# The last feature block by halves of the tokens, without Pool

## The chip, the cores and the metric

The kernel runs on one core of a Trainium2 chip. The metric is the device time of that core in microseconds, the median of several runs. The engines are TensorE (PE in the profile, with PEld for its weight loads), VectorE (DVE), ScalarE (ACT), GpSimd (POOL) and SyncE (SP), which issues all the DMAs here.

## What is computed

One layer of a diffusion backbone over 256 latent tokens and 256 context tokens, 1024 features wide: a gated feed-forward half step, a token mixer of retention and Fourier branches, a second gated feed-forward half step for the latent tokens, and a norm over the features. The change touches the end of it:

```python
x = x + 0.5 * g3x * swiglu(modulate(rmsnorm(x, norm_ffn2[l]), sh3x, sc3x), w13_ffn2[l], w2_ffn2[l])
...
return rmsnorm(x, norm_final)

def swiglu(h, w13, w2):
    a, b = jnp.split(h @ w13, 2, axis=-1)
    return (jax.nn.silu(a) * b) @ w2

def rmsnorm(x, w):
    xf = x.astype(jnp.float32)
    y = xf * lax.rsqrt(jnp.mean(xf * xf, axis=-1, keepdims=True) + EPS)
    return (y * w.astype(jnp.float32)).astype(x.dtype)
```

The hidden width of the feed-forward part is 2816.

## The kernel before

Features lie on the 128 partitions and tokens along the free axis. The 1024 features are `KT` = 8 blocks, the hidden width `MT` = 22 blocks of 128. The residual stream is `xs[j]`, 128 partitions by 512 columns, context tokens first and latent tokens behind (`T` = 256 each).

All large products are made from three fp32r products (`mm3`, lines 95 to 97): the weights and the moving operand are each split into a high and a low part, and low weights by high data, high by low, and high by high are summed in PSUM. A product loads its 128x128 weights anew each time. `load_w` brings weights in: a DMA on SP (line 84), a cast on ScalarE (line 85), a subtraction on VectorE (line 86). Squares are summed over the features by a product with `ones`, in plain f32; such a product leaves two records in the trace.

The last stage is the second matrix of the second feed-forward part. For each feature block `j`, `w2_chunks` brings 22 blocks of weights in three pieces, 66 products of 256 columns fill the bank `z`, and `y_evac` (line 467, VectorE) adds it, times a gate, to `xs[j]`. For the blocks 0 to 6, `add_sq` then squares the block (line 461, ScalarE) and adds the square to `ssum` (line 462, VectorE), and ScalarE writes the block times its norm weight to `xw` (line 1052). All of that lies beside the products of the next block. For block 7 nothing comes after: the sum of the seven squares goes through PE in the middle of its products (line 1047), and then one thing follows the other. ScalarE squares the last block (line 1054), PE adds that to the sum (line 1055), `rstd_of` takes the root on ScalarE (line 233) and the reciprocal on VectorE (line 235), and `xw` is multiplied by it in three groups of blocks, 6 and 7 on Pool, 0 to 2 and 3 to 5 on VectorE (line 1061), each stored by a DMA of its own (line 1062).

Two other places show up below. Line 269, in the opening, multiplies f32 data of 128 columns; line 306 multiplies f32 data of two columns; line 631 turns blocks of fp32r data over by a product with the unit matrix, in the transpose form of the product, with 128 columns. The order of the instructions on each engine is set by a scheduler when the program is built, within what the code's dependences allow.

Of the kernel before, what the change touches and what calls it, by code (L numbers as in the profile page):

```python
# [7 lines left out]
F32 = mybir.dt.float32  # L8
F32R = mybir.dt.float32r
BF16 = mybir.dt.bfloat16  # L10
AF = mybir.ActivationFunctionType
ALU = mybir.AluOpType

P = 128
T = 256
D = 1024
KT = D // P
FF = 2816
MT = FF // P
# [6 lines left out]
T2K = 4  # L26
# [8 lines left out]
BIAS, NRM, GNW, DEC = 0, 72, 104, 120  # L35
# [4 lines left out]
def block_kernel(ctx: ExitStack, tc: tile.TileContext, i: dict, out: bass.AP):  # L40
    nc = tc.nc
    V, S, G, PE = nc.vector, nc.scalar, nc.gpsimd, nc.tensor

    def pool(name, bufs=1, **kw):
        return ctx.enter_context(tc.tile_pool(name=name, bufs=bufs, reuse_waits="tile", **kw))
# [3 lines left out]
    tp = pool("tp")  # L49
# [16 lines left out]
    def bank(name):  # L66
        return psum.tile([P, 512], F32, name=name, tag="ps")
# [9 lines left out]
    def load_w(src, n, lo_engine=None, at=0):  # L77

        uid[0] += 1
        raw, hi, lo = [wtile(t, f"{t}{uid[0]}")[:, at : at + n] for t in ("wr", "wh", "wl")]  # L80
        dst = raw
        if len(src.shape) == 3:
            dst = dst.rearrange("p (k c) -> p k c", k=src.shape[1])
        nc.sync.dma_start(dst, src)
        S.copy(hi, raw)  # L85
        (lo_engine or V).tensor_tensor(lo, raw, f32(hi), op=ALU.subtract)  # L86
        return hi, lo
# [5 lines left out]
    def mm3(o, w, a, start, stop):  # L93

        PE.matmul(o, w[1], a[0], start=start, stop=False)  # L95
        PE.matmul(o, w[0], a[1], start=False, stop=False)  # L96
        PE.matmul(o, w[0], a[0], start=False, stop=stop)  # L97

    def sl(pair, *idx):
        return pair[0][idx], pair[1][idx]  # L100
# [11 lines left out]
    start = ExitStack()  # L112
# [11 lines left out]
    ones = per.tile([P, P], F32, name="ones")  # L124
# [14 lines left out]
    sm = per.tile([P, N_SMALL], F32, name="sm")  # L139
# [11 lines left out]
    xs, first_ada, first_w = [], {}, {}  # L151
# [31 lines left out]
    for n, c in enumerate(ch):  # L183
        for q in range(4):
            r = slice(32 * q, 32 * q + 1)
# [41 lines left out]
    def gate_col(st, s, k):  # L227
        return gate[:, s, st * KT + k : st * KT + k + 1]

    def rstd_of(ps_ap, width, name):  # L230

        sd = tp.tile([P, T], F32, name=f"sd{name}", tag="sd", bufs=1)
        S.activation(sd[:, :width], ps_ap, AF.Sqrt, bias=eps)
        r = tp.tile([P, T], F32, name=f"rstd{name}", tag="rstd", bufs=2)
        V.reciprocal(r[:, :width], sd[:, :width])
        return r[:, :width]
# [4 lines left out]
    for k in range(KT):  # L241
        if k < T2K:
            sq = tp.tile([P, 512], F32, name=f"sq1_{k}", tag="t2k", bufs=T2K)
        else:
            sq = stp.tile([P, 512], F32, name=f"sq1_{k}", tag=f"at{k % 2}" if k < 6 else "xr", bufs=1 + (k > 5))
# [10 lines left out]
        for q in range(4):  # L256
            PE.matmul(
                ps_st[32 * q : 32 * q + 32, :P], ones[:, :32], sq[:, q * P : (q + 1) * P],
                start=(k == 0), stop=(k == KT - 1), skip_group_check=True, tile_position=(0, 32 * q),
# [82 lines left out]
    def gated_unit(pa, pb, name):  # L342
        sa = tp.tile([P, 512], F32, name=f"sa{name}", tag="t2k", bufs=T2K)
        S.activation(sa, pa, AF.Silu)
        V.tensor_tensor(sa, sa, pb, op=ALU.mult)
        gg = (
            gp.tile([P, 512], F32R, name=f"gh{name}", tag="gh", bufs=HALF),
            gp.tile([P, 512], F32R, name=f"gl{name}", tag="gl", bufs=HALF),
        )
        split(gg[0], gg[1], sa)  # L350
        return gg
# [66 lines left out]
    g = [gated_unit(acc[2 * m], acc[2 * m + 1], f"1_{m}") for m in range(M1)]  # L418
# [25 lines left out]
    def w2_chunks(src, kts, at=0):  # L444
        ws, k0 = [], 0
        for n in kts:
            w = load_w(src[:, k0 * P : (k0 + n) * P], n * P, at=at)
            ws += [sl(w, slice(None), slice(c * P, (c + 1) * P)) for c in range(n)]
            k0 += n
        return ws  # L450

    ssum = [None]

    def add_sq(ap, cols, first, name):

        sq = tp.tile([P, 512], F32, name=f"sq{name}", tag="t2k", bufs=T2K)
        w = cols.stop - cols.start
        if first:
            S.activation(ssum[0][:, cols], ap, AF.Square)
            return  # L460
        S.activation(sq[:, :w], ap, AF.Square)
        V.tensor_tensor(ssum[0][:, cols], ssum[0][:, cols], sq[:, :w], op=ALU.add)

    def y_evac(ps, j, streams, st, col0):
        for n, s in enumerate(streams):
            c = slice(s * T, (s + 1) * T)
            V.scalar_tensor_tensor(
                xs[j][:, c], ps[:, col0 + n * T : col0 + (n + 1) * T], gate_col(st, s, j),
                xs[j][:, c], op0=ALU.mult, op1=ALU.add,
            )  # L470
# [45 lines left out]
    g = []  # L516
# [228 lines left out]
    def o_unit(hd, us):  # L745
        pss = [bank(f"o{hd}_{n}") for n in range(4)]
        for n in range(4):
            w = v_weights(hd, n)
            for k in (2 * n, 2 * n + 1):
                u = sl(us[k // 2], slice(None), slice((k % 2) * T, (k % 2 + 1) * T))  # L750
                for d in range(4):
                    c = (k % 2) * DV + d * P
                    mm3(pss[d][:, :T], sl(w, slice(None), slice(c, c + P)), u, k == 0, k == KT - 1)
        sq = [tp.tile([P, 512], F32, name=f"os{hd}_{n}", tag="t2k", bufs=T2K) for n in range(2)]
        for d in range(4):
            S.activation(sq[d // 2][:, (d % 2) * T : (d % 2 + 1) * T], pss[d][:, :T], AF.Square)
        G.tensor_tensor(sq[0], sq[0], sq[1], op=ALU.add)
        for d in range(4):
            c = slice((d % 2) * T, (d % 2 + 1) * T)
            S.copy(tt[2 * hd + d // 2][:, c], pss[d][:, :T])  # L760
        return sq[0]
# [106 lines left out]
    sq = None  # L868
    for hd in range(HEADS):
# [20 lines left out]
        sq = o_unit(hd, us)  # L890
# [19 lines left out]
    for j in range(KT):  # L910
        ws = [load_w(i["wgate"][j, c], 1024) for c in range(2)]
# [7 lines left out]
        for k in range(2 * KT):  # L919
            c = (k % 8) * P  # L920
# [33 lines left out]
    XC = slice(T, 2 * T)  # L954
# [49 lines left out]
    def raw_unit(m, pa, pb):  # L1004
        r = rstd3[0]
        cc = tp.tile([P, 2], F32, name=f"cc{m}", tag="cc", bufs=4)
        V.tensor_copy(cc[:, 0:1], pa[:, T : T + 1])
        V.tensor_copy(cc[:, 1:2], pb[:, T : T + 1])
        a = tp.tile([P, 512], F32, name=f"a2_{m}", tag="t2k", bufs=T2K)
        V.tensor_tensor(a[:, :T], pa[:, :T], r, op=ALU.mult)  # L1010
        S.activation(a[:, :T], a[:, :T], AF.Silu, bias=cc[:, 0:1])
        V.tensor_tensor(a[:, T:], pb[:, :T], r, op=ALU.mult)
        V.scalar_tensor_tensor(a[:, :T], a[:, T:], cc[:, 1:2], a[:, :T], op0=ALU.add, op1=ALU.mult)
        gg = g2_tiles(m)
        split(gg[0], gg[1], a[:, :T])
        return gg
# [11 lines left out]
    g = [raw_unit(m, *first[m]) for m in range(2)]  # L1028
# [7 lines left out]


    ssum[0] = per.tile([P, 512], F32, name="ssum4", tag="ssum")
    pf = bank("st4")
    xw = g2.tile([P, KT, T], F32, name="xw")  # L1040
    for j in range(KT):
        ws = w2_chunks(i["w2b"][j], (8, 8, 6))
        py = bank(f"z{j}")
        for k in range(MT):
            mm3(py[:, :T], ws[k], g[k], k == 0, k == MT - 1)
            if (j, k) == (KT - 1, 8):
                PE.matmul(pf[:, :T], ones, ssum[0][:, :T], start=True, stop=False)
        y_evac(py, j, (1,), 2, 0)
        if j < KT - 1:
            add_sq(xs[j][:, XC], slice(0, T), j == 0, f"4_{j}")  # L1050
            c = NRM + 3 * KT + j
            S.mul(xw[:, j, :], xs[j][:, XC], sm[:, c : c + 1])
    sq = tp.tile([P, 512], F32, name="sq4_last", tag="t2k", bufs=T2K)
    S.activation(sq[:, :T], xs[KT - 1][:, XC], AF.Square)
    PE.matmul(pf[:, :T], ones, sq[:, :T], start=False, stop=True)
    r = rstd_of(pf[:, :T], T, "4")
    c = NRM + 4 * KT - 1
    S.mul(xw[:, KT - 1, :], xs[KT - 1][:, XC], sm[:, c : c + 1])
    for j0, j1, engine in ((6, 8, G), (0, 3, V), (3, 6, V)):
        rb = r.unsqueeze(1).to_broadcast([P, j1 - j0, T])  # L1060
        engine.tensor_tensor(xw[:, j0:j1, :], xw[:, j0:j1, :], rb, op=ALU.mult)
        nc.sync.dma_start(out[:, j0:j1, :], xw[:, j0:j1, :])


# [102 lines left out]
```

## Time and profile before

| | |
|---|---|
| median of 3 runs | 988.46 us (988.08 to 989.26) |
| profiled execution, its time | 986.11 us |
| its span | 984.3 us |
| PE busy in the span | 957.3 us (97%) |
| VectorE busy | 658.1 us (67%) |
| ScalarE busy | 468.1 us (48%) |
| Pool busy | 37.7 us (4%) |

The profiled execution is one of its own and not one of the three runs. Times in the rows are microseconds from the start of its span unless marked ns. Products on PE are pipelined: the records of two of them overlap, so the spacing of their starts, and not the length of a record, is what a product costs. The chain of work that ended last is followed back from the last instruction, at each step to what released it.

### The profile page before, as it was taken

What the parts mean: (1) busy time and instruction counts of PE and PEld (TensorE: products, weight loads), DVE (VectorE), ACT (ScalarE), POOL (GpSimd) and SP (SyncE); (2) the same over time, 40 slices, a digit from 0 to 9 for tenths busy, and PEclk for the clock granted to TensorE, in tenths of its full rate; (3) what the DMA queues carried; (4) which work ended last, traced back from release to release, by engine and by line L of the source; (5) the groups of instructions that cost most, each with busy time, mean ns of one, the idle gap of its engine ahead of it and who ended that gap; (6) DMA issues with size and microseconds to landing.
All of it is one profiled execution on the core that took longest, in us unless ns stands there. A gap on an engine that the chain in (4) does not pass through costs nothing.

```text
span 984.3 us, 16732 instructions
## 1 busy us (share of the span) xinstructions
PE 957.3 (97%) x6792; PEld 881.2 (90%) x6792; DVE 658.1 (67%) x1056; ACT 468.1 (48%) x733; POOL 37.7 (4%) x21
## 2 busy tenths in 40 slices
PE   6999999999999999899999999899999999999996
PEld 4778888888888889899999999899999999999995
DVE  7879999998333433966765646975555688555553
ACT  5444322224422432755665647755444566555541
POOL 0000000000000001200000006200000000000000
PEclk9999999999999999999999999999999999999998
DMA  8757766995332232323231526356656565666661
GB/s 348 238 203 235 235 195 214 352 391 195 97 109 67 78 99 86 97 87 121 95 130 44 157 81 186 117 175 201 192 189 199 174 190 175 211 198 186 199 190 43
DMA packets 49237, 166.84 MB, mean 169 GB/s; under 512 B 5380, under 2 KB 7044, under 8 KB 49160
## 3 DMA queue, kind: packets, MB, share of 16 engines
q1 hardware_dynamic: 49160, 165.77, 52.4%
q8 instruction: 53, 0.87, 0.3%
q14 instruction: 24, 0.20, 0.1%
HBM read 164.70 MB, written 1.05 MB: 168 GB/s over the span
## 4 chain that ended last, share of the span: by engine, by line
PE 93%; DVE 3%; ACT 1%; DMA 1%; issue 1%; DVEq 0%; SPq 0%; ACTq 0%
PE y L95 4%; PE y L97 4%; PE y L96 4%; PE pa L97 4%; PE pb L95 4%; PE pa L95 4%; PE pb L97 4%; PE pa L96 3%; PE pb L96 3%; PE ro L97 2%; PE ro L95 2%; PE ro L96 2%; PE fb L97 2%; PE fa L97 2%; PE fb L96 2%; PE fa L96 2%
## 5 line engine op out<-in xcount | busy, mean ns | idle before, releaser
L86 DVE TENSOR_TENSOR wl<-wr,wh 128x1024 fp32r<-128x1024 f32 (+1 forms) x214 | 248.7, 1163 | 190.4 <-ACT wh L85 189.5
L85 ACT CAST wh<-wr 128x1024 fp32r<-128x1024 f32 (+1 forms) x226 | 227.3, 1007 | 273.7 <-PE y L97 79.2
L198 DVE CUSTOM_DVE_ANT_0 junk<-ada,cb,sm 128x1024 bf16<-128x1024 f32 x96 | 123.0, 1281 | 6.5 <-DMA ada<-in_ada 4.9
L96 PE MATMUL y<-gl,wh 128*128 128x512 f32 (+1 forms) x198 | 72.4, 366 | 0.0
L95 PE MATMUL y<-gh,wl 128*128 128x512 f32 (+1 forms) x198 | 72.3, 366 | 0.0
L97 PE MATMUL y<-gh,wh 128*128 128x512 f32 (+1 forms) x198 | 72.2, 365 | 0.0
L97 PE MATMUL pa<-h1h,wh 128*128 128x512 f32 x152 | 59.2, 389 | 0.0
L96 PE MATMUL pa<-h1l,wh 128*128 128x512 f32 x152 | 59.2, 389 | 0.0
L95 PE MATMUL pa<-h1h,wl 128*128 128x512 f32 x152 | 59.2, 389 | 0.0
L95 PE MATMUL pb<-h1h,wl 128*128 128x512 f32 x152 | 59.2, 389 | 0.0
L96 PE MATMUL pb<-h1l,wh 128*128 128x512 f32 x152 | 59.2, 389 | 0.0
L97 PE MATMUL pb<-h1h,wh 128*128 128x512 f32 x152 | 59.1, 389 | 0.0
L96 PE MATMUL z<-g2l,wh 128*128 128x256 f32 x176 | 48.8, 277 | 0.0
L97 PE MATMUL z<-g2h,wh 128*128 128x256 f32 x176 | 48.6, 276 | 0.0
L95 PE MATMUL z<-g2h,wl 128*128 128x256 f32 x176 | 48.6, 276 | 0.0
L86 POOL TENSOR_TENSOR wl<-wr,wh 128x1024 fp32r<-128x1024 f32 x12 | 29.9, 2515 | 439.2 <-ACT wh L85 439.2
L96 PEld LDWEIGHTS y<-gl,wh 128*128 128x128 f32 x198 | 37.3, 188 | 6.1
L95 PEld LDWEIGHTS y<-gh,wl 128*128 128x128 f32 x198 | 37.2, 188 | 6.0
L97 PEld LDWEIGHTS y<-gh,wh 128*128 128x128 f32 x198 | 37.2, 188 | 6.0
L97 PE MATMUL fb<-hnh,wh 128*128 128x256 f32 x144 | 39.8, 276 | 0.0
L96 PE MATMUL fb<-hnl,wh 128*128 128x256 f32 x144 | 39.8, 276 | 0.0
L97 PE MATMUL fa<-hnh,wh 128*128 128x256 f32 x144 | 39.8, 276 | 0.0
(336 smaller groups left out, 2903.1 us busy)
## 6 DMA issues: line engine op xcount, KB each, us to landing
ada<-in_ada SPq DMA_DIRECT2D x72, 512.0 KB, 5.2
wr<-in_w13b SPq DMA_DIRECT2D x44, 512.0 KB, 4.4
wr<-in_w13a SPq DMA_DIRECT2D x38, 512.0 KB, 4.4
wrv<-in_wv SPq DMA_DIRECT2D x16, 512.0 KB, 4.5
wr<-in_wg SPq DMA_DIRECT2D x16, 512.0 KB, 4.1
wr<-in_wgate SPq DMA_DIRECT2D x16, 512.0 KB, 4.4
wr<-in_pret SPq DMA_DIRECT2D x16, 512.0 KB, 4.1
wr<-in_w2b SPq DMA_DIRECT2D x16, 512.0 KB, 3.8
```

What stands on the lines that cost most here:

```text
L85: S.copy(hi, raw)
L86: (lo_engine or V).tensor_tensor(lo, raw, f32(hi), op=ALU.subtract)
L95: PE.matmul(o, w[1], a[0], start=start, stop=False)
L96: PE.matmul(o, w[0], a[1], start=False, stop=False)
L97: PE.matmul(o, w[0], a[0], start=False, stop=stop)
L198: V.tensor_tensor_reduce(junk, raw, cb[:, s, :], 1.0, sm[:, BIAS + n : BIAS + n + 1], ALU.mult, ALU.add, mod[:, s, n : n + 1],)
```

## The change

Blocks 0 to 6 of the last stage stay as they are, but for the multiplication by the norm weight, which moves into a helper. Block 7 is computed in two halves of 128 tokens. Each half has banks of its own for the product (`z7_0`, `z7_1`) and for the sum of squares (`st4_0`, `st4_1`), 66 products of 128 columns with the same weights, its own add, square, sum, root and reciprocal, and then all eight blocks of `xw` for its 128 tokens are multiplied in two groups of four, both on VectorE, and stored by two DMAs. Pool has no part in it. A store takes, on each partition, four pieces of 128 elements.

```diff
+    def weighted(j, c):
+        n = NRM + 3 * KT + j
+        S.mul(xw[:, j, c], xs[j][:, T + c.start : T + c.stop], sm[:, n : n + 1])
+
-    for j in range(KT):
+    for j in range(KT - 1):
         ws = w2_chunks(i["w2b"][j], (8, 8, 6))
         py = bank(f"z{j}")
         for k in range(MT):
             mm3(py[:, :T], ws[k], g[k], k == 0, k == MT - 1)
-            if (j, k) == (KT - 1, 8):
-                PE.matmul(pf[:, :T], ones, ssum[0][:, :T], start=True, stop=False)
         y_evac(py, j, (1,), 2, 0)
...
-    sq = tp.tile([P, 512], F32, name="sq4_last", tag="t2k", bufs=T2K)
-    S.activation(sq[:, :T], xs[KT - 1][:, XC], AF.Square)
-    PE.matmul(pf[:, :T], ones, sq[:, :T], start=False, stop=True)
-    r = rstd_of(pf[:, :T], T, "4")
-    c = NRM + 4 * KT - 1
-    S.mul(xw[:, KT - 1, :], xs[KT - 1][:, XC], sm[:, c : c + 1])
-    for j0, j1, engine in ((6, 8, G), (0, 3, V), (3, 6, V)):
-        rb = r.unsqueeze(1).to_broadcast([P, j1 - j0, T])
-        engine.tensor_tensor(xw[:, j0:j1, :], xw[:, j0:j1, :], rb, op=ALU.mult)
-        nc.sync.dma_start(out[:, j0:j1, :], xw[:, j0:j1, :])
+    j = KT - 1
+    ws = w2_chunks(i["w2b"][j], (8, 8, 6))
+    for n in range(2):
+        c = slice(n * P, (n + 1) * P)
+        py, pf = bank(f"z{j}_{n}"), bank(f"st4_{n}")
+        for k in range(MT):
+            mm3(py[:, :P], ws[k], sl(g[k], slice(None), c), k == 0, k == MT - 1)
+            if k == 12:
+                PE.matmul(pf[:, :P], ones, ssum[0][:, c], start=True, stop=False)
+        x = xs[j][:, T + n * P : T + (n + 1) * P]
+        V.scalar_tensor_tensor(x, py[:, :P], gate_col(2, 1, j), x, op0=ALU.mult, op1=ALU.add)
+        sq = tp.tile([P, 512], F32, name=f"sq4_last{n}", tag="t2k", bufs=T2K)
+        S.activation(sq[:, :P], x, AF.Square)
+        PE.matmul(pf[:, :P], ones, sq[:, :P], start=False, stop=True)
+        r = rstd_of(pf[:, :P], P, f"4_{n}")
+        weighted(j, c)
+        for j0 in range(0, KT, 4):
+            rb = r.unsqueeze(1).to_broadcast([P, 4, P])
+            V.tensor_tensor(xw[:, j0 : j0 + 4, c], xw[:, j0 : j0 + 4, c], rb, op=ALU.mult)
+            nc.sync.dma_start(out[:, j0 : j0 + 4, c], xw[:, j0 : j0 + 4, c])
```

On PE, the end of the program before. `z` is the bank of block 7, `g2h` and `g2l` the gated hidden blocks, `wh` and `wl` the two parts of the weights; the number at the end is the size of the moving operand.

```order
L97 MATMUL z_10445<-g2h_9721,wh_10440 128x256
L95 MATMUL z_10445<-g2h_9790,wl_10441 128x256
L96 MATMUL z_10445<-g2l_9791,wh_10440 128x256
L97 MATMUL z_10445<-g2h_9790,wh_10440 128x256
L1055 MATMUL st_9796<-sq_last,ones 128x256
```

On PE after the change, the place inside the products of half 1 (`z_1`) where the squares of half 0 are summed:

```order
L95 MATMUL z_1_10526<-g2h_8893,wl_10434 128x128
L96 MATMUL z_1_10526<-g2l_8894,wh_10433 128x128
L97 MATMUL z_1_10526<-g2h_8893,wh_10433 128x128
L1067 MATMUL st_0_10445<-sq_last_10514,ones 128x128
L95 MATMUL z_1_10526<-g2h_8962,wl_10434 128x128
```

The sum over the last squares stood behind all products; that of half 0 now stands behind 27 of the 66 products of half 1 (the sum of half 1 stands last, as before).

On VectorE, the end of the program before, from the last weight piece on:

```order
L86 TENSOR_TENSOR wl_10441<-wr_10439,wh_10440 128x768
L467 SCALAR_TENSOR_TENSOR xs_112<-z_10355,gate,xs_112 128x256
L462 TENSOR_TENSOR ssum_9795<-ssum_9795,sq_6_10423 128x256
L467 SCALAR_TENSOR_TENSOR xs_112<-z_10445,gate,xs_112 128x256
L235 RECIPROCAL rstd_10519<-sd_10517 128x256
L1061 TENSOR_TENSOR xw<-xw,rstd_10519 128x768 x2
```

And after the change:

```order
L462 TENSOR_TENSOR ssum_9795<-ssum_9795,sq_6_10422 128x256
L1064 SCALAR_TENSOR_TENSOR xs_112<-z_0_10444,gate,xs_112 128x128
L235 RECIPROCAL rstd_0_10519<-sd_0_10517 128x128
L1072 TENSOR_TENSOR xw<-xw,rstd_0_10519 128x4x128 x2
L1064 SCALAR_TENSOR_TENSOR xs_112<-z_1_10526,gate,xs_112 128x128
L235 RECIPROCAL rstd_1_10601<-sd_1_10599 128x128
L1072 TENSOR_TENSOR xw<-xw,rstd_1_10601 128x4x128 x2
```

Add, reciprocal and multiplies of half 0 stand ahead of those of half 1. On SP four stores stand where three stood, all behind the last weight load.

## Rows read from the trace of the kernel before

**Rows 1.** Page, part 1: busy time, share of the span, instructions of each engine.

```profile
PE 957.3 (97%) x6792; PEld 881.2 (90%) x6792; DVE 658.1 (67%) x1056; ACT 468.1 (48%) x733; POOL 37.7 (4%) x21
```

**Rows 2.** Stretches, PE alone: length, busy (records), granted clock, DMA share, GB/s.

```profile
13.20:14.20 1.00, 0.96 (x8) 1.00 1.01 406
966.00:974.00 8.00, 8.00 (x69) 1.00 0.01 2
```

**Rows 3.** Timeline of PE, first and last product of z7: start, length, record.

```profile
965.91 0.28 PE L95 MATMUL z<-g2h,wl 128*128 128x256 f32 x1
...
973.73 0.28 PE L97 MATMUL z<-g2h,wh 128*128 128x256 f32 x1
```

**Rows 4.** Chain that ended last, 973 to 985 us: start, length, what.

```profile
974.05 0.49 DVE xs L467
...
974.56 0.42 ACT sq_last L1054
...
975.03 0.71 PE st L1055 x2
...
975.77 0.48 ACT sd L233
...
976.27 1.76 DVE rstd L235
...
978.06 0.96 DVE xw L1061
979.02 1.94 DVEq L1161
```

**Rows 5.** Timeline of all engines, 978 to 984.4 us.

```profile
978.06 2.90 DVE L1061 TENSOR_TENSOR xw<-xw,rstd 128x768 f32<-128x768 f32 x2
978.17 1.97 POOL L1061 TENSOR_TENSOR xw<-xw,rstd 128x512 f32<-128x512 f32 x1 [356.07 <-DVE rstd L235]
```

**Rows 6.** Waits of SP from 975 us on: total, times, longest.

```profile
SPq L1161 <- DMA out_xT<-xw: 1.9, 1, 1.9
```

**Rows 7.** Timeline of the weight loads, 13 to 14.4 us.

```profile
13.24 0.97 PEld L269 LDWEIGHTS rs<-rstd1q,pick 128*128 128x128 f32 x8 [1.93 <-DVE rstd1q L235]
14.13 0.36 PEld L284 LDWEIGHTS tr<-unit_raw,ada 128*128 128x128 f32 x3
```

**Rows 8.** Chain that ended last, 23 to 25 us; `acc` has 512 columns.

```profile
23.74 0.12 PE tr L306 x2
23.86 0.34 PE acc L95
24.20 0.23 PE acc L96
```

**Rows 9.** Groups of weight loads by shape: busy us, mean ns, idle before.

```profile
L95 PEld LDWEIGHTS z<-g2h,wl 128*128 128x128 f32 x176 | 33.0, 188 | 0.0
...
L631 PEld LDWEIGHTS ht<-unit,h2xh 128*128 128x128 f32 x16 | 1.7, 142 | 0.0
...
L269 PEld LDWEIGHTS rs<-rstd1q,pick 128*128 128x128 f32 x8 | 1.0, 191 | 1.9 <-DVE rstd1q L235 1.9
```

**Rows 10.** Chain that ended last, 413 to 420 us.

```profile
413.85 1.16 PE ht L631 x14
```

**Rows 11.** Groups of VectorE by shape: busy us, mean ns, idle before.

```profile
L769 DVE TENSOR_TENSOR tt<-tt,rstdo 128x512 f32<-128x512 f32 x8 | 5.1, 683 | 0.0
...
L235 DVE RECIPROCAL rstd1q<-sd1q 128x128 f32<-128x128 f32 x1 | 1.0, 953 | 0.1
```

**Rows 12.** Groups of ScalarE by shape.

```profile
L233 ACT ACTIVATE sd1q<-st,eps 128x128 f32<-128x128 f32 x1 | 0.4, 368 | 1.2 <-PE st L257 1.2
```

**Rows 13.** DMAs of the whole span: issues, KB each, median us to landing.

```profile
out_xT<-xw SPq DMA_DIRECT2D x2, 384.0 KB, 2.5
...
unit_raw<-in_unit SPq DMA_DIRECT2D x1, 64.0 KB, 1.8
```

**Rows 14.** DMAs of 43 to 50 us, two loads in pieces of 1 KB.

```profile
wr<-in_w13a SPq DMA_DIRECT2D x2, 512.0 KB, 4.1
```

More of the change, by code (lines that the diff above doesn't have):

```diff
@@ L1038, in block_kernel @@
     ssum[0] = per.tile([P, 512], F32, name="ssum4", tag="ssum")
-    pf = bank("st4")
     xw = g2.tile([P, KT, T], F32, name="xw")
-    for j in range(KT):
+    def weighted(j, c):
+        n = NRM + 3 * KT + j
+        S.mul(xw[:, j, c], xs[j][:, T + c.start : T + c.stop], sm[:, n : n + 1])
+    for j in range(KT - 1):
         ws = w2_chunks(i["w2b"][j], (8, 8, 6))
@@ L1045, in block_kernel @@
             mm3(py[:, :T], ws[k], g[k], k == 0, k == MT - 1)
-            if (j, k) == (KT - 1, 8):
-                PE.matmul(pf[:, :T], ones, ssum[0][:, :T], start=True, stop=False)
         y_evac(py, j, (1,), 2, 0)
[L1049 to L1052, printed above, removed]
-    sq = tp.tile([P, 512], F32, name="sq4_last", tag="t2k", bufs=T2K)
-    S.activation(sq[:, :T], xs[KT - 1][:, XC], AF.Square)
-    PE.matmul(pf[:, :T], ones, sq[:, :T], start=False, stop=True)
-    r = rstd_of(pf[:, :T], T, "4")
-    c = NRM + 4 * KT - 1
-    S.mul(xw[:, KT - 1, :], xs[KT - 1][:, XC], sm[:, c : c + 1])
-    for j0, j1, engine in ((6, 8, G), (0, 3, V), (3, 6, V)):
-        rb = r.unsqueeze(1).to_broadcast([P, j1 - j0, T])
-        engine.tensor_tensor(xw[:, j0:j1, :], xw[:, j0:j1, :], rb, op=ALU.mult)
-        nc.sync.dma_start(out[:, j0:j1, :], xw[:, j0:j1, :])
+        add_sq(xs[j][:, XC], slice(0, T), j == 0, f"4_{j}")
+        weighted(j, slice(0, T))
+    j = KT - 1
[18 more added lines that the diff above has]
+            nc.sync.dma_start(out[:, j0 : j0 + 4, c], xw[:, j0 : j0 + 4, c])
 def _layout(a):
```

## The prediction

> **What bounds the kernel now.** The page first: PE is busy for 97% of the span and loads weights, on the row PEld, for 90% of it; Pool does next to nothing [rows 1]. The change touches only the last 18 us, so everything else is read there. In 966 to 974 us PE has no idle time at a granted clock of 1.00, its 2.4 GHz level [rows 2]. That is the last feature block, z7: its first product starts at 965.91 and its last at 973.73, 66 products of 256 columns and the two records of the sum st [rows 3]. With one more spacing of 0.113 us PE spends 7.93 us on it. What follows is a chain with one link at a time [rows 4]: VectorE adds z to xs (0.49), ScalarE squares (0.42), PE sums the squares (0.71), ScalarE takes the root (0.48), VectorE the reciprocal (1.76), then multiplies six of the eight blocks in two steps, 0.96 and 1.94 us. The second step does what the first does and takes twice as long; Pool multiplies the other two blocks from 978.17 for 1.97 us, the same stretch [rows 5]. The last store is issued after the second step, and SP then waits 1.9 us for it [rows 6]. From the start of the add at 974.05 to the end of the span at 984.3 that is 10.3 us in which PE computes for 0.7.
>
> So the end has two parts: 7.93 us limited by PE, and 10.3 us limited by a chain. The change pays in the first to shorten the second.
>
> **Part 1, the products by halves.** The 66 products of 256 columns become 132 of 128, with the same multiplications in all, but each product has its own load of 128 columns of weights, so the loads double too. The question is whether a load hides behind a product of half the length. No fp32r product in this trace has under 256 columns, so the price comes from the nearest rows. The sums by L269 have 128 columns and a weight load for each record: eight loads start from 13.24 us on, and the next one, of L284, at 14.13, so 0.89 / 8 = 0.111 us each, again at a clock of 1.00 [rows 2, 7]. These are f32 products in two records, where the product itself might hold up the next one. The products by L306 settle that: they have two columns, practically no multiplication, and yet the two records and the product behind them take 0.12 + 0.34 us where the next ones take 0.23 each, so (0.46 - 0.23) / 2 = 0.115 us each [rows 8]. A load of fp32r weights for z and a load for L269 last the same, 188 and 191 ns [rows 9]. I take from this that a new 128x128 load can start only every 0.11 us, that 256 columns (0.113) just cover it, and that 128 columns do not. Price: 0.111 us a product whatever its width, with 0.108 and 0.1135 as its ends (a little below the two rows, and the spacing of today).
>
> After the change PE runs 132 products and, ahead of the last sum, six records of st (two halves of ssum, and the squares of half 0), 138 loads: 138 x 0.111 = 15.32 us. **PE: 15.32 - 7.93 = +7.39 us**, with the ends +6.97 and +7.73. All of it lies on the path, since nothing else is late in 966 to 974.
>
> The nearest rows on the cheap side are the transposes by L631, also 128 columns with own weights in fp32r: 14 of them take 1.16 us, 0.083 each [rows 10]. Their loads last 142 ns and not 188 [rows 9], so they are another kind of load; I leave them to a rival. The Trainium skill, page "TensorE: Matmul & The Clock Gate", section "Back-to-back issue gap", gives about 81 ns per product for sustained pairs of load and product of 128 columns. By that rule PE would pay 138 x 0.081 - 7.93 = +3.2 us, an estimate from that page. It speaks against my price, the transposes agree with it, and the loads of the kind that z uses do not.
>
> **Part 2, half 0 in the cover of half 1.** In the order PE meets the squares' sum of half 0 only after 27 products of z_1, 29 records on: 3.2 us, in which VectorE's add and ScalarE's square (under 0.9 us together) are long done. So PE does not wait there. Root, reciprocal and two multiplies of half 0 then take some 3 us: they are done some 6.3 us into the 7.9 that z_1 and its sums last. VectorE is free for half 1, and the two stores of half 0 are issued 2 us before z_1 ends. Cost zero, hidden by z_1; that cover would be gone only with a spacing under 0.07 us, and would then cost about 0.6 us.
>
> **Part 3, the chain behind half 1.** Each link has 128 columns in place of 256. The add: a VectorE step of 768 elements takes 0.96 us [rows 4] and one of 512 takes 0.683 [rows 11], 1.07 ns an element, so -0.13. The root has 0.368 in its one row of 128 columns, at the opening [rows 12], against 0.48: -0.10; the square on the same engine likewise, -0.11. The sum: two records of two passes each, 128 columns less for each of two passes in the record that holds up the other, -0.21. The reciprocal has 0.953 at the opening [rows 11], against 1.76: -0.80. The two multiplies: 512 elements each at 0.683 [rows 11], back to back with 0.08 of overlap, 1.29 us, against 2.90 for the two of today [rows 5]: -1.61. This is the largest term: 1.06 of it is the slowing of the second step beside Pool (1.94 against the first one's 0.96 less the overlap), the rest fewer elements. The last store: 256 KB in pieces of 512 B where today it is 384 KB in pieces of 3 KB. The trace has 2.5 us for today's, 1.8 for 64 KB in pieces of 512 B [rows 13], and 4.1 for the two loads of 512 KB in pieces of 1 KB [rows 14]; I take 2.5 again, because bytes go down and pieces up, with ends 1.9 and 3.5. **Chain: -2.97 us**, ends -3.5 and -1.9.
>
> The store on SP comes last in its queue, and no load stands behind it. Pool's removal costs nothing elsewhere: VectorE does 2 x 512 elements a half, half of that in the cover of z_1.
>
> **Sum.** +7.39 - 2.97 = +4.42 us. Against the profiled execution, 986.11 us with a span of 984.3, that is 990.5; that execution lies 2.35 below the median of the runs, 988.46, so I add the change to the median: **992.9 us, 0.45% slower**. Its own range is 991.9 (6.97 - 3.5) to 994.3 (7.73 - 1.9).
>
> **Rivals.** Each goes by the spacing s of a 128-column product: time = 988.46 + 138 s - 7.93 - 2.97. It decides at 0.079 us: above that the change loses. All other terms are too small to turn the sign.
>
> *Faster: loads hide behind 128 columns.* If the load streams at the speed of the product, s is half of 0.113, 0.057 us. PE then pays nothing (138 x 0.057 = 7.87), and the chain's -2.97 stands, less the 0.6 us by which half 0 would now hold VectorE: -2.4, **986.1 us**. For it: 512 columns (0.23 [rows 8]) and 256 (0.113 [rows 3]) stand in the ratio of their columns, so at 256 the load shows nowhere. Against it: the two-column products at 0.115 [rows 8]. Chance 5%.
>
> *Much the same: loads as cheap as those of the transposes.* s = 0.083 gives 11.45 - 7.93 - 2.97 = +0.55, **989.0 us**. For it: the only fp32r products of 128 columns in the trace run so [rows 10]. Against it: the shorter load of those [rows 9]. The rule of the skill named above falls here, +0.3 us by its figure. Chance 9%.
>
> *Far slower: a narrow fp32r product is run as an f32 product,* in two records. L269's four products take 0.223 each [rows 7]: 132 x 0.223 + 6 x 0.111 = 30.1, so 30.1 - 7.93 - 2.97 = +19.2, **1007.7 us**. For it: every fp32r product that multiplies has at least 256 columns here, so nothing excludes it. Against it: the transposes of that type and width have one record each [rows 10]. Chance 10%.
>
> That halves do not overlap is excluded by the order: VectorE's reciprocal and multiplies of half 0 stand ahead of the add of half 1, and PE's sum of half 0 inside z_1.
>
> **How the numbers follow.** The forecast has 76%. The range goes from the rival of equal time to a little over the forecast's own top: 988.9 to 994.5, which leaves out the faster case, the f32 case and the forecast's fringes. About 0.2%, 2 us, is what a measurement of this kernel can tell from no change: s below 0.064 is faster (5%), 0.064 to 0.093 the same (9%, and 1% for a forecast with its ends against it), the rest slower (85%).
>
> **What would show it.** In the new profile: PE products of z_0 and z_1 at a spacing of 0.11 us with loads of 188 ns; z7's stretch at 15.3 us, ending near 981.1; VectorE's chain of half 0 finished before the last product of z_1; the chain after it 7.3 us long, with two multiplies of 0.69; one record for each product. A spacing of 0.08 or 0.06 proves the price wrong, 264 records instead of 132 the third rival right; a last store over 3.5 us would break the chain's term.

## The result: 993.0 us, 0.43% slower

The changed kernel takes 993.01 us in the median of 4 runs (992.15 to 993.92), the kernel before beside it 988.40 (988.08 to 989.26): a ratio of 1.0043, with a 95% interval of 1.0031 to 1.0056. The prediction, 992.9 us, and its sign hold. The profiled execution took 992.15 us with a span of 990.1.

That span is 5.8 us longer than before's, but 1.04 of this is there before the changed code runs: z7 begins at 966.95 where before has 965.91 [rows 3]. In all the profiles of this study that start lies between 965.9 and 970.8 us, in kernels that do the same work up to there, so the time of one execution says little about a change of 0.5 us. Everything below is therefore counted from z7's first product, in two pieces: to the start of the last add (products), and from there to the end of the span (chain). An experiment without a ratio was executed once, and only its trace is read.

| | products | chain | of it, from the end of the last multiply | sum |
|---|---|---|---|---|
| before | 8.14 | 10.29 | 3.38 | 18.43 |
| after | 15.56 | 7.60 | 3.64 | 23.15 |
| difference | +7.42 | -2.69 | +0.26 | +4.73 |

The page, part 1, answers to [rows 1]:

```profile
PE 966.9 (98%) x6862; PEld 891.8 (90%) x6862; DVE 657.9 (66%) x1060; ACT 469.2 (47%) x736; POOL 35.6 (4%) x20
```

PE has 70 records more and is busy for 9.6 us more: 7.42 of it in z7's stretch (15.52 against 8.10), -0.21 in the last sum, and 2.4 ahead of z7, in work that is alike in both. VectorE does as much as before, Pool one multiply less. Then stretches: the products of half 0, those of half 1, and the chain. The columns are length, then busy time (instructions) of PE, weight loads, VectorE, ScalarE and Pool, the granted clock, the DMA share and GB/s.

```profile
966.95:974.30 7.35, 7.35 (x69) 7.35 (x67) 0.94 (x3) 0.82 (x2) 0.00 (x0) 1.00 0.00 0
974.70:982.20 7.50, 7.50 (x70) 7.50 (x69) 2.59 (x4) 0.97 (x3) 0.00 (x0) 1.00 0.16 44
982.50:990.10 7.60, 0.49 (x2) 0.30 (x2) 2.60 (x4) 0.97 (x3) 0.00 (x0) 0.69 0.31 83
```

PE has no idle time in either half, at a clock of 1.00 as in [rows 2], and the load row is as full as the product row. Half as much arithmetic per product, and as many products per microsecond as before. Timeline of PE around the seam, and the last product; it answers to [rows 3]:

```profile
966.84 0.28 PE L97 MATMUL z<-g2h,wh 128*128 128x256 f32 x1
966.95 0.22 PE L95 MATMUL z<-g2h,wl 128*128 128x128 f32 x1
967.01 0.28 PE L96 MATMUL z<-g2l,wh 128*128 128x128 f32 x1
967.12 0.27 PE L97 MATMUL z<-g2h,wh 128*128 128x128 f32 x1
...
982.19 0.28 PE L97 MATMUL z<-g2h,wh 128*128 128x128 f32 x1
```

From the first to the last are 137 steps (132 products and six records of sums) in 15.24 us, 0.111 each. Only the first narrow product, behind a wide one, starts the next after 0.06. The weight loads keep their step of 0.11 across the seam: they start at 966.84, 966.95, 967.06 and 967.17.

The chain that ended last, from the last add on (start, length, what), answers to [rows 4], with SP's wait for the last store, which answers to [rows 6]:

```profile
982.51 0.36 DVE xs L1064
...
982.89 0.32 ACT sq_last L1066
...
983.25 0.50 PE st L1067 x2
...
983.78 0.38 ACT sd L233
...
984.18 0.96 DVE rstd L235
...
985.17 0.69 DVE xw L1072
985.86 0.60 DVEq L1172
```

```profile
SPq L1172 <- DMA out_xT<-xw: 2.1, 1, 2.1
```

Every link is shorter, the second multiply (on the engine's queue in the last row, 0.60) is as quick as the first, and only the wait for the store has grown, from 1.9 to 2.1.

VectorE on the way there:

```profile
978.38 0.95 DVE L235 RECIPROCAL rstd<-sd 128x128 f32<-128x128 f32 x1 [3.33 <-ACT sd L233]
979.37 1.29 DVE L1072 TENSOR_TENSOR xw<-xw,rstd 128x512 f32<-128x512 f32 x2
982.51 0.35 DVE L1064 SCALAR_TENSOR_TENSOR xs<-z,gate,xs 128x128 f32<-128x128 f32 x1 [1.85 <-PE z L97]
```

Half 0 is multiplied at 980.66, and VectorE then waits 1.85 us for the products of half 1: half 0 costs nothing.

### The profile page after: what moved, and what is told of

Its sections match the earlier page's. It is cut to its first block, busy times and chain, and to the rows that moved or that the text cites. A ratio compares the mean times of both kernels' runs of the same rounds, so it can differ in the third digit from the quotient of the medians.

```text
span 990.1 us, 16880 instructions
## 1 busy us (share of the span) xinstructions
PE 966.9 (98%) x6862; PEld 891.8 (90%) x6862; DVE 657.9 (66%) x1060; ACT 469.2 (47%) x736; POOL 35.6 (4%) x20
## 4 chain that ended last, share of the span: by engine, by line
PE 93%; DVE 2%; ACT 2%; DMA 1%; issue 1%; SPq 0%; DVEq 0%; ACTq 0%
PE y L95 4%; PE y L96 4%; PE y L97 4%; PE pa L97 3%; PE pa L96 3%; PE pb L96 3%; PE pb L97 3%; PE pa L95 3%; PE pb L95 3%; PE z L97 2%; PE z L96 2%; PE z L95 2%; PE ro L95 2%; PE ro L96 2%; PE ro L97 2%; PE fa L97 2%
## 5 line engine op out<-in xcount | busy, mean ns | idle before, releaser
L95 PE MATMUL z<-g2h,wl 128*128 128x256 f32 (+1 forms) x198 | 54.6, 276 | 0.0
L96 PE MATMUL z<-g2l,wh 128*128 128x256 f32 (+1 forms) x198 | 54.6, 276 | 0.0
L97 PE MATMUL z<-g2h,wh 128*128 128x256 f32 (+1 forms) x198 | 54.6, 276 | 0.0
```

## Experiments

### The two parts of the change, each alone

**Products only.** Halves on PE, before's tail with Pool.

```diff
+        if j == KT - 1:
+            for n in range(2):
+                c = slice(n * P, (n + 1) * P)
+                py = bank(f"z{j}_{n}")
+                for k in range(MT):
+                    mm3(py[:, :P], ws[k], sl(g[k], slice(None), c), k == 0, k == MT - 1)
...
+                V.scalar_tensor_tensor(x, py[:, :P], gate_col(2, 1, j), x, op0=ALU.mult, op1=ALU.add)
+            continue
...
```

> Block 7's products by halves alone (132 products of 128 columns, two adds); square, sum, root, reciprocal, multiplies and stores as in the kernel before, with Pool. My theory, a weight load every 0.111 us: z7's stretch is 134 records, 14.9 us against 7.9 before, and the chain from the last add on 10.16 us against 10.29 (an add of 128 columns): +6.8 us in all, 0.7% slower than before and 2.1 slower than the changed kernel. If loads hid behind 128 columns, z7 would stay at 7.9 and the whole be equal to before.

Measured: 996.14 us against 988.39, ratio 1.0075 (1.0059 to 1.0090). Products 15.32, chain 10.17, sum 25.50: +7.07 against before. With Pool still in the tail, VectorE's two multiplies take 0.96 and 1.93 us, as in [rows 4].

**Tail only.** Products of 256 columns, norm and stores by halves, no Pool.

```diff
+    py = bank(f"z{j}")
+    pfs = [bank(f"st4_{n}") for n in range(2)]
+    for k in range(MT):
+        mm3(py[:, :T], ws[k], g[k], k == 0, k == MT - 1)
...
     for n in range(2):
...
-            mm3(py[:, :P], ws[k], sl(g[k], slice(None), c), k == 0, k == MT - 1)
...
+        V.scalar_tensor_tensor(x, py[:, c], gate_col(2, 1, j), x, op0=ALU.mult, op1=ALU.add)
```

> The other part alone: block 7's products stay 66 of 256 columns, and add, square, sum, root, reciprocal, multiplies and stores go by halves without Pool. z7's stretch 7.9 us as before. Chain: VectorE starts the reciprocal of half 0 some 1.65 us after the first add, then has 0.99 + 1.29 + 0.99 + 1.29 to do without a gap, so its last multiply ends 6.2 us after the first add, against 6.9 before; the store in pieces of 512 B takes 3.6 from there to the end of the span where that before took 3.3. Sum 9.85 against 10.29, -0.4 us: not to be told from before by its time, only by its profile. If halves cost as such (more instructions, smaller pieces), it is slower than before.

Measured: ratio 0.9999 (0.9989 to 1.0009). The trace shows what the time can't: sum 18.03, -0.40 against before. Its VectorE:

```profile
977.48 0.61 DVE L1067 SCALAR_TENSOR_TENSOR xs<-z,gate,xs 128x128 f32<-128x128 f32 x2 [6.55 <-PE z L97]
979.24 0.95 DVE L235 RECIPROCAL rstd<-sd 128x128 f32<-128x128 f32 x1 [1.15 <-ACT sd L233]
980.23 1.29 DVE L1075 TENSOR_TENSOR xw<-xw,rstd 128x512 f32<-128x512 f32 x2
981.44 0.95 DVE L235 RECIPROCAL rstd<-sd 128x128 f32<-128x128 f32 x1
```

Both halves now stand one behind the other on VectorE, with nothing to cover the first.

The two parts alone come to +7.07 - 0.40 = +6.67, the whole change to +4.73. The missing -1.94 exists only when both are there: with the products by halves, half 0's reciprocal and multiplies leave the end and lie in half 1's products. That is the purchase, and the products cost 7.4 for it.

### What Pool did to VectorE

```diff
-    for j0, j1, engine in ((6, 8, G), (0, 3, V), (3, 6, V)):
+    for j0, j1, engine in ((6, 8, V), (0, 3, V), (3, 6, V)):
```

> The kernel before with one word changed: the multiply of blocks 6 and 7 goes to VectorE instead of Pool. If Pool is what slows VectorE's second multiply of 768 (1.94 us against 0.96), all three now run at 1.07 ns an element: 0.61 + 0.88 + 0.96 = 2.45 us against 2.90, so the chain is 9.85 against 10.29, -0.45 us. If the slow second multiply has another cause (its store, its place), the three take 0.61 + 0.96 + 1.94 = 3.5 and the kernel is 0.6 us slower.

Measured: ratio 0.9999 (0.9989 to 1.0009), sum 18.09, -0.34. VectorE's three multiplies and the chain through them:

```profile
980.97 2.43 DVE L1061 TENSOR_TENSOR xw<-xw,rstd 128x512 f32<-128x512 f32 x3
```

```profile
980.97 0.69 DVE xw L1061
981.66 0.87 DVEq L1161
982.53 0.87 DVE xw L1061
```

VectorE does all eight blocks in 2.43 us, less than the 2.90 it took for six beside Pool [rows 5]. A step of 768 elements takes 0.87 behind another one and 1.94 while Pool multiplies: Pool's two blocks cost VectorE more than doing them. The multiplies are 0.47 shorter, as expected; the end behind the last of them is 0.13 longer (3.51 against 3.38), hence -0.34 and not -0.45. The rows of before fit a wait as well as a slow step: Pool's multiply ends at 980.14 [rows 5], and VectorE's second step ends 0.82 later, about the 0.87 that it takes without Pool. Which of the two it is, no run takes apart.

### Is it the load that sets 0.111?

If the weight load sets the spacing, a product of any width up to 256 costs the same; if it is the product, in two passes, half the columns take half.

```diff
-            mm3(py[:, :P], ws[k], sl(g[k], slice(None), c), k == 0, k == MT - 1)
+            mm3(py[:, :64], ws[k], sl(g[k], slice(None), slice(n * P, n * P + 64)), k == 0, k == MT - 1)
...
```

> The changed kernel with products of 64 columns in block 7: 64 of each half's 128 tokens are left out of the product and its add. This parts two theories of the 0.11 us. A load of weights every 0.111 us whatever the width: z7's stretch stays 15.3 us. The rival, narrow fp32r products run at half the rate, two passes over their columns: 64 columns take 0.057 and the stretch is 132 x 0.057 + 6 x 0.111 = 8.2 us.

Measured: 1002.42 us, worse than anything here. Products of 64 columns, early and later:

```profile
968.15 0.28 PE L97 MATMUL z<-g2h,wh 128*128 128x64 f32 x1
968.26 0.28 PE L95 MATMUL z<-g2h,wl 128*128 128x64 f32 x1
...
974.03 0.40 PE L96 MATMUL z<-g2l,wh 128*128 128x64 f32 x1
974.24 0.40 PE L97 MATMUL z<-g2h,wh 128*128 128x64 f32 x1
```

```profile
968.20:973.20 5.00, 5.00 (x48) 5.00 (x46) 0.91 (x2) 0.82 (x2) 0.00 (x0) 1.00 0.00 0
975.00:981.00 6.00, 6.00 (x30) 6.00 (x30) 0.29 (x1) 0.60 (x2) 0.00 (x0) 0.50 0.00 0
```

At a clock of 1.00 a product of 64 columns is spaced by 0.11, the same as one of 128. That excludes the two passes, for which half the columns take half. What neither side expected is the second stretch: the granted clock is 0.50, the 1.2 GHz level, and the spacing 0.213, though PE has no idle time in the rows before. Products and chain come to 24.80 + 7.83.

Two widths in one kernel, with the whole computation, test the flatness again:

```diff
-        c = slice(n * P, (n + 1) * P)
+        c = slice(*((0, 192), (192, T))[n])
+        N = c.stop - c.start
...
-            mm3(py[:, :P], ws[k], sl(g[k], slice(None), c), k == 0, k == MT - 1)
+            mm3(py[:, :N], ws[k], sl(g[k], slice(None), c), k == 0, k == MT - 1)
...
```

> The changed kernel with halves of unequal width: 192 tokens first, then 64; nothing is left out. A load of weights every 0.111 us whatever the width: products of 192 columns also stand 0.111 to 0.113 apart, the first part takes 66 + 2 records x 0.112 = 7.6 us, and the price of the division is the same for any place of the cut. If the cost went by columns with a surcharge for narrow ones, 192 columns would stand at 0.16 to 0.17 and the first part take 11 us. In the second part, 64 columns as in the run with 64, the granted clock may fall to its 1.2 GHz level again, and the spacing with it to 0.213; the chain behind it is 1.5 us shorter than that of equal halves (reciprocal -0.4, multiplies -0.55, add, square, sum and root -0.4 together).

Measured: 995.13 us; 18.11 + 6.31 = 24.42. PE in the 192 columns, then early in the 64:

```profile
970.05 0.28 PE L95 MATMUL z<-g2h,wl 128*128 128x192 f32 x1
970.16 0.28 PE L96 MATMUL z<-g2l,wh 128*128 128x192 f32 x1
...
977.01 0.28 PE L95 MATMUL z<-g2h,wl 128*128 128x64 f32 x1
977.12 0.28 PE L96 MATMUL z<-g2l,wh 128*128 128x64 f32 x1
```

0.11 at 192 columns, 0.11 at 64, and 0.21 once the clock has fallen again (983.05 to 983.26 us, at a granted clock of 0.50). So 64, 128 and 192 columns cost the same as 256, which excludes a price by columns under 256. A fixed price of a narrow product, load or no load, would look the same so far; the rows of the next run part the two.

### Fewer loads

The high weights multiply both parts of the data. With the two parts side by side, one product of 2 x 128 columns does for two loads' worth, and 88 loads remain of 132.

```diff
-            mm3(py[:, :P], ws[k], sl(g[k], slice(None), c), k == 0, k == MT - 1)
+            both_parts = py[:, : 2 * P].rearrange("p (x l) -> p x l", x=2)
+            PE.matmul(both_parts, ws[k][0], g[k][2][:, :, c], start=k == 0, stop=False)
+            PE.matmul(py[:, :P], ws[k][1], g[k][0][:, c], start=False, stop=k == MT - 1)
...
-        V.scalar_tensor_tensor(x, py[:, :P], gate_col(2, 1, j), x, op0=ALU.mult, op1=ALU.add)
+        for p in range(2):
+            V.scalar_tensor_tensor(x, py[:, p * P : (p + 1) * P], gate_col(2, 1, j), x, op0=ALU.mult, op1=ALU.add)
```

> The changed kernel, but the high weights of block 7 are loaded once for the low and the high part of the data: one product of 2 x 128 columns into two column ranges, which two adds on VectorE bring into xs, instead of two products of 128. Multiplications are the same, loads are 88 where the changed kernel has 132 and the kernel before 66. If loads are the price, z7's stretch is 44 x (0.113 + 0.111) + 6 x 0.111 = 10.5 us against 15.35; with 0.3 more for the second add the chain is 7.9. In all 4.5 us less than the changed kernel, 0.45%, and 0.2 us more than the kernel before, not to be told from it by time. If the price is one for narrow products as such, the 44 of 128 columns still pay it and the wide ones pay for their columns, and the result is the same 10.5; if it lies in the count of instructions or in the division itself, the stretch stays near 15.

Measured: 989.38 us against 988.03, ratio 1.0018 (1.0009 to 1.0027). The products do as expected, 10.7 us for the stretch. Against a count of instructions that time is no evidence, though the expectation takes it for such: the products fall from 132 to 88 as the loads do, so a fixed price of each would give 10.5 as well. The order of starts is evidence. Products, then loads, of one stretch:

```profile
967.43 0.22 PE L1063 MATMUL z<-g,wl 128*128 128x128 f32 x1
967.49 0.33 PE L1062 MATMUL z<-g,wh 128*128 128x256 f32 x1
967.66 0.22 PE L1063 MATMUL z<-g,wl 128*128 128x128 f32 x1
```

```profile
967.43 0.19 PEld L1062 LDWEIGHTS z<-g,wh 128*128 128x128 f32 x1
967.54 0.19 PEld L1063 LDWEIGHTS z<-g,wl 128*128 128x128 f32 x1
967.66 0.19 PEld L1062 LDWEIGHTS z<-g,wh 128*128 128x128 f32 x1
```

A product of 128 columns lets the next one start after 0.06 us, and the wide one takes the remaining 0.17, while the loads start every 0.11 to 0.12 throughout. The first narrow product behind a wide one shows the same in the other kernels: the next starts after 0.03 us at 64 columns, 0.06 at 128 and 0.08 at 192. So a narrow product is cheap in itself; it is the load that comes no faster than every 0.11 us, and that is the price.

But the sum is 20.09, +1.67 against before. VectorE, and PE's last steps:

```profile
976.71 0.95 DVE L235 RECIPROCAL rstd<-sd 128x128 f32<-128x128 f32 x1 [3.47 <-ACT sd L233]
977.69 1.29 DVE L1076 TENSOR_TENSOR xw<-xw,rstd 128x512 f32<-128x512 f32 x2
978.90 0.73 DVE L1068 SCALAR_TENSOR_TENSOR xs<-z,gate,xs 128x128 f32<-128x128 f32 x2
```

```profile
977.71 0.22 PE L1063 MATMUL z<-g,wl 128*128 128x128 f32 x1
980.03 0.80 PE L1071 MATMUL st<-sq_last,ones 128*128 128x128 f32 x2 [2.10 <-ACT sq_last L1070]
```

The cover is gone: PE has started its last product at 977.71, and VectorE is in half 0's multiplies until 978.9, so the add starts 11.81 us after z7's first product and not 10.9. PE stands idle for 2.1 us meanwhile, and its sum then takes 0.80, at a granted clock of 0.50 in that stretch, where the changed kernel has 0.50 us at a clock of 1.00. To see the cover's share alone, half 0's two multiplies are left out of the same kernel:

```diff
-            V.tensor_tensor(xw[:, j0 : j0 + 4, c], xw[:, j0 : j0 + 4, c], rb, op=ALU.mult)
+            if n:
+                V.tensor_tensor(xw[:, j0 : j0 + 4, c], xw[:, j0 : j0 + 4, c], rb, op=ALU.mult)
```

> The run with one load for both parts, with the two multiplies of half 0 by its reciprocal left out (half 0 is stored without them), to free VectorE under half 1. In that run the add of half 1 starts 11.81 us after z7's first product, though its last product starts at 10.62; the add follows products by 0.31 elsewhere. If VectorE's work for half 0 is what is in the way, the add now starts at 10.95, 0.87 earlier, and the sum from z7's first product to the end of the span falls from 20.1 to 19.2 (18.9 if PE's last sum no longer falls into the lower clock). If PE's bank is late for another reason, the add stays at 11.8.

Measured: 988.25 us. Products 10.88, chain 8.00, sum 18.87:

```profile
978.48 0.74 DVE L1068 SCALAR_TENSOR_TENSOR xs<-z,gate,xs 128x128 f32<-128x128 f32 x2 [0.31 <-PE z L1063]
```

```profile
979.61 0.49 PE L1071 MATMUL st<-sq_last,ones 128*128 128x128 f32 x2 [1.17 <-ACT sq_last L1070]
```

The add waits for PE again, the sum is back at 0.49, and 1.22 us of the 1.67 are gone. The 0.45 that is left says that with stores in pieces of 512 B the halves don't pay, even with a third of the loads gone and half 0's multiplies costing nothing. With the larger pieces of the next section, worth 0.52 us, the sum would be 18.35 against 18.43, about even; that is an estimate.

### The last store

From the end of the last multiply to the end of the span the change takes 0.26 us more than before, with fewer bytes. First the pieces, by an output laid out so that a half's four blocks are 2 KB on the DRAM side:

```diff
-OUT = (P, KT, T)
+OUT = (2, P, KT, P)
...
-            nc.sync.dma_start(out[:, j0 : j0 + 4, c], xw[:, j0 : j0 + 4, c])
+            nc.sync.dma_start(out[n, :, j0 : j0 + 4, :], xw[:, j0 : j0 + 4, c])
```

> The changed kernel with an output laid out by halves in memory, so that a store's piece on a partition is 2 KB and not 512 B; nothing else differs. In the changed kernel 3.64 us pass from the last multiply's end to the end of the span, in the one before 3.38. If the small pieces are the reason, 3.3 to 3.4 here; if it is the second store beside it, 3.6 as before the edit.

Measured: 995.72 us, products 15.56, chain 7.60, 3.64 at the end: nothing moved, which seemed to speak against the pieces. Then the fixed part of a store, with one store for half 1 in place of two:

```diff
-            nc.sync.dma_start(out[:, j0 : j0 + 4, c], xw[:, j0 : j0 + 4, c])
+            if n == 0:
+                nc.sync.dma_start(out[:, j0 : j0 + 4, c], xw[:, j0 : j0 + 4, c])
+        if n:
+            nc.sync.dma_start(out[:, :, c], xw[:, :, c])
```

> The changed kernel, with half 1 stored by one DMA of 512 KB behind both multiplies instead of two of 256 KB. From the last multiply's end to the end of the span the changed kernel takes 3.64 us. If what counts there is that the first store still holds the DMA engines, a part of its bytes is already moved before the last multiply ends and one store of 512 KB is slower, 4.0 to 4.3. If each store pays mainly for itself, fixed, the single one takes 3.6 or less.

Measured: 992.12 us, and 4.58 at the end, above both expectations. So it is no fixed cost, and the bytes weigh more than thought: 256 KB more behind the last multiply take 0.94. The DMA rows from 975 us on show that the first test had tested nothing. Packets of the kernel with the new output layout (the changed kernel's row is the same), and of before; the mean rate in them is over a window longer than the stores:

```profile
DMA packets 2112, 1.05 MB, mean 39 GB/s; under 512 B 64, under 2 KB 2112, under 8 KB 2112
```

```profile
DMA packets 432, 1.05 MB, mean 39 GB/s; under 512 B 48, under 2 KB 48, under 8 KB 432
```

The output's layout left the store at 2112 small packets, because the pieces in `xw` were still 512 B. So `xw` too was laid out by halves (the edit is shown against the run with the new output layout):

```diff
-    xw = g2.tile([P, KT, T], F32, name="xw")
+    xw = g2.tile([P, 2, KT, P], F32, name="xw")
...
-            nc.sync.dma_start(out[n, :, j0 : j0 + 4, :], xw[:, j0 : j0 + 4, c])
+            nc.sync.dma_start(out[n, :, j0 : j0 + 4, :], xw[:, n, j0 : j0 + 4, :])
```

> Changed block 7 with stores whose pieces are 2 KB on both sides. In the run whose output alone was laid out by halves the store still left as 2,112 packets of under 2 KB, because the pieces were still 512 B in xw, so that run changed nothing that it meant to change. Here xw too is laid out by halves, each half's four blocks in one piece. Products and chain up to the last multiply as in the changed kernel: 15.56 us from the first product to the last add, 3.95 us from there to the end of the last multiply. If the size of the pieces is why the end took 3.64 us from the last multiply on where before had 3.38 with more bytes: about 400 packets instead of 2,112 and 3.2 to 3.4 us. If the size of the pieces does not matter: 3.64 again.

Measured: 992.61 us; products 15.56, and 3.12 at the end. Its packets, issues (KB, median us to landing) and SP's wait, and then the issues of the changed kernel:

```profile
DMA packets 576, 1.05 MB, mean 39 GB/s; under 512 B 64, under 2 KB 64, under 8 KB 576
...
out_xT<-xw SPq DMA_DIRECT2D x4, 256.0 KB, 2.1
```

```profile
SPq L1173 <- DMA out_xT<-xw: 1.6, 1, 1.6
```

```profile
out_xT<-xw SPq DMA_DIRECT2D x4, 256.0 KB, 2.5
```

It is the pieces: 576 packets land in 2.1 us, 2112 in 2.5, and the end is 0.52 shorter. The rate tells where most of that lies. A stretch in the middle of half 1's stores, first in the changed kernel and then in this one (the last two columns are the DMA share and GB/s):

```profile
987.00:988.50 1.50, 0.00 (x0) 0.00 (x0) 0.00 (x0) 0.00 (x0) 0.00 (x0) 0.50 1.08 287
988.00:989.00 1.00, 0.00 (x0) 0.00 (x0) 0.00 (x0) 0.00 (x0) 0.00 (x0) 0.50 1.03 385
```

The DMA engines are full in both. At 287 and 385 GB/s the 512 KB of half 1 take 1.83 and 1.36 us, an estimate from these rows: 0.47 of the 0.52. In the Trainium skill, page "DMA: Bandwidth & Descriptors", section "Specifications", 512 B is the size from which transfers go at line rate. These runs differ: 287 GB/s in pieces of 512 B, 385 in pieces of 2 KB.

### What was worth keeping

The tail by halves without Pool, behind products of 256 columns, with stores of 2 KB on both sides:

```diff
-    xw = g2.tile([P, KT, T], F32, name="xw")
+    xw = g2.tile([P, 2, KT, P], F32, name="xw")
...
+    py = bank(f"z{j}")
+    pfs = [bank(f"st4_{n}") for n in range(2)]
+    for k in range(MT):
+        mm3(py[:, :T], ws[k], g[k], k == 0, k == MT - 1)
...
-            nc.sync.dma_start(out[:, j0 : j0 + 4, c], xw[:, j0 : j0 + 4, c])
+            nc.sync.dma_start(out[n, :, j0 : j0 + 4, :], xw[:, n, j0 : j0 + 4, :])
```

> What the other runs left worth having: block 7 with products of 256 columns as before, the norm and the stores by halves without Pool, and the stores in pieces of 2 KB on both sides. If the gains add up: 8.1 us for the products, 9.9 less the 0.5 that the larger pieces gave, so 17.5 us from the first product of block 7 to the end, 0.9 less than before, and a time of 0.999 of before, at the edge of what can be told apart. If the stores of half 0 now hold up those of half 1, since both halves' stores come within 3.2 us: 18.0 us as in the run with 512-byte pieces, and the same time as before.

Measured: 986.82 us against 988.38, ratio 0.9985 (0.9975 to 0.9994). Products 8.15, chain 9.36 with 3.13 at its end, sum 17.51 where before has 18.43. The gains add up, and this kernel is faster than both.

## Why the prediction was right

**The spacing of a narrow product** was the term that decided. Taken: 0.111 from the f32 loads of [rows 7], bounded by the two-column products of [rows 8]. Measured: 0.111. The widths of 64 and 192 show that it does not go by columns, and the order of starts in the fewer-loads kernel that it is the load, as was argued; the predicted +7.39 us are +7.42.

**The rivals below it fall.** Spacings of 0.057 and 0.083 occur nowhere between the changed kernel's products behind the first one. The 81 ns that the Trainium skill gives for pairs of load and product (page "TensorE: Matmul & The Clock Gate", section "Back-to-back issue gap") do not hold for these products: 0.111 at the same 128 columns. The transposes of [rows 10] were rightly left aside for their shorter load [rows 9]. The third rival, narrow fp32r products run as f32, falls too: z7 has one record for each product.

**Half 0 in the cover** costs nothing, as said: VectorE is idle for 1.85 us before half 1's add. The fewer-loads kernel shows the condition that the prediction named: at 10.7 us for both halves the cover is short.

**The chain up to the last multiply** came out link by link: 0.36, 0.32, 0.50, 0.38, 0.96 and 1.29 us; from the add to the end of the multiplies 3.95 us, as its terms give. That Pool caused the 1.94 of [rows 5] was read from the overlap of two rows; the run without Pool shows it.

**The last store was mis-sized.** The step "I take 2.5 again, because bytes go down and pieces up" set the two against each other and let them cancel. The pieces weigh more: +0.26 us, so the chain gives -2.69 and not -2.97. The row it rested on [rows 13] also joined two stores; the last of before has 2.4. The end taken, 3.5 us to landing, was wide enough. With this term +4.42 becomes +4.68, against +4.73 measured. That the time itself, 992.9, comes within 0.1 us of 993.01 is in part luck: the trace puts the change 0.31 us above the forecast, the medians 0.19 (4.61).

Expectations failed in the experiments too. The 64 columns were costed without a fall of the clock. The chain behind a last part of 64 columns came out 1.29 us shorter than that of equal halves and not 1.5, with its sum at the lower clock (0.70 us). The fewer-loads kernel was costed by PE alone (+0.2 for +1.67), with the cover that the change itself needed left out of the sum. The first test of the pieces changed one side of the store only, and the single store of half 1 came out above both of its cases.

What stays open: why small packets go at the lower rate, what lowers the granted clock in a stream of 64-column products, and whether VectorE's step beside Pool runs slowly or waits.

## What to carry to other kernels

Splitting a product along its moving side multiplies the weight loads, and where a load of 128x128 fp32r can start only every 0.111 us, products under 256 columns with a load each save nothing: count loads, not multiplications. A split pays if what it hides at the end exceeds the extra loads, and only while the cover is longer than what is put into it, so a faster cover needs its own sum. For a store, look at the packets: here pieces of 512 B in SBUF alone kept them small, whatever the layout in DRAM, and laying out the tile in SBUF anew gave 0.52 us for the same bytes.

## What the hardware did that was not expected

- In the stream of 64-column products the granted clock went from 1.00 to 0.50 at about 973.2 us, with no idle time of PE in the 5 us before; the spacing went from 0.11 to 0.213. In the 192-and-64 kernel it fell within the 64-column part too. The changed kernel's products of 128 columns kept 1.00 through 15 us. At the 1.2 GHz level a 64-column product costs about twice as much, and z7's stretch took 24.80 us against 15.56.
- Pool's multiply of 512 elements took 1.97 us, and the second VectorE step beside it took 1.94 where 0.87 is its time behind another step without Pool.
- Stores in 512-byte pieces landed in 2.5 us where 2 KB pieces took 2.1, for the same 256 KB.
